# One core, RWKV layer: the mixed streams of k formed and issued ahead of the two low-rank paths

## The chip, the core and the metric

The kernel runs on one core of one Trainium2 chip: TensorE (PE in the rows, its weight loads PEld), VectorE (DVE), ScalarE (ACT), GpSimd (POOL) and a queue that issues the transfers (SP). The metric is the device time of one execution in microseconds, as the median of several; three runs of the kernel before gave 2172.70, 2178.46 and 2179.18 us.

## The reference, cut to what matters

Four post-norm layers work on 256 context tokens and 256 latent tokens of 1024 features: retention, mLSTM, RWKV-7, retention. The change lies at the start of the RWKV layer. There each token stream `u` is mixed with a shifted copy of itself, six times with six weights, and projected:

```
xx = shifted - u
xr, xw, xk, xv, xa, xg = (u + xx * mix[j] for j in range(6))
r, k, v, g = einsum('nbtd,nde->nbte', stack([xr, xk, xv, xg]), w_rkvg)
kk = heads(k * k_k);  kk = kk / max(sqrt(sum(kk * kk)), 1e-12)
wlog = -softplus(-(w0[d] + tanh(xw @ w1[d]) @ w2[d])) - 0.5     # d: two directions
a    = sigmoid(a0[d] + (xa @ a1[d]) @ a2[d])
```

The context is shifted along its sequence, the latents on a grid of rows of 64. The "two low-rank paths" are `tanh(xw @ w1)` and `xa @ a1`, both directions together 128 columns wide each. They are needed only later, when the recurrence over chunks of 64 tokens is prepared; k and its normalised form are needed there too.

## The kernel before

Features lie on partitions (8 tiles of 128), the 512 tokens along the free dimension: 0 to 255 the context, 256 to 511 the latents. `Norm.finish` (lines 103 to 119) of the layer in front writes the RWKV layer's input `h`, first for the context, then for the latents, tile by tile on DVE (lines 108, 110), POOL (108) and ACT (116). `rk_project` (line 1031) then does this:

- `shifted` (1040) forms `xx` for one stream: subtractions on DVE (1037), edges on ACT (1038).
- `mixed` (1068) gives one tile of one mixed stream in float32, on DVE (line 1070), into a slot `rxm`. There are three such slots, and `colb` and `lnpart` of the norm take theirs from the same three.
- `lora` (1084) sends 8 such tiles of a stream through TensorE in plain float32 (line 1087) for each of the two paths, and ACT takes the sums to `tw` and `ta` (1088). Plain float32 matmuls leave two records each in the trace.
- `mix_split` (1073) forms the k stream's tiles and splits each into two exact parts: the high one on ACT (line 288), the low one on DVE (line 289). The tiles are named `szr`, `xk` and `zh` after the slots they take (2, 3 and 3 pairs).
- `first_proj` (268) multiplies them with the first two units of k's weights, three matmuls for each pair (lines 256 to 258): four tiles of output, of the context's 256 tokens first, then of the latents', 96 matmuls for each half.
- The other four tiles of k (numbers 4 to 7) follow over all 512 tokens, 24 matmuls each (`proj`, "pp" in the rows). For each four tiles: copy out (1113), store to memory (1114), times `k_k` into a slot `kkt` (1115; four slots), square (1118), sums over a head (1120), root and reciprocal (1122 to 1124), spread back (1128), multiply (1130), store (1131). A slot `kkt` is free again once its store has landed.

The sums of both paths, `lps`, take two banks of PSUM of a tag "ps" that has two, and keep them until ACT has read them. `rk_rest` (1134) follows with r's mixed stream (line 1144, then 288 and 289) and its projection, and `rk_core` with the recurrence: `prep` (1268; its POOL lines are 1315, 1320 and 1322), `solve` (1363; POOL and DVE in step, lines 1380 and 1381, eight times), `whole`, `step`.

No order is written out by hand here: the framework's scheduler lays the calls of each engine out by a simulation of its own, in the order of the program where nothing else decides. Each engine then works its list off strictly in that order.

Of the kernel before, what the change touches and what calls it, by code (L numbers as in the profile page):

```python
# [16 lines left out]
T = 512  # L17
# [31 lines left out]
class Norm:  # L49
    """The layer's norm of one stream over its features, taken up tile by tile. The sums are of the differences to the  # L50
    mean of the first 128 features, which is within a few standard deviations of the mean."""
# [17 lines left out]
    def add(self, c):  # L69
# [10 lines left out]
        # four partial sums, each on 32 partitions  # L80
# [22 lines left out]
    def finish(self):  # L103
# [16 lines left out]
        # the last layer adds to the latents alone  # L120
# [3 lines left out]
    def late(self):  # L124
        """What the next layer adds to."""
        nc = self.net.nc
        for k in range(KT):
            x = self.x[k]
            nc.gpsimd.tensor_tensor(out=x, in0=x, in1=self.rs, op=OP.mult)
            nc.gpsimd.tensor_scalar(out=x, in0=x, scalar1=self.cs[:, 2, k:k + 1], scalar2=self.cs[:, 3, k:k + 1], op0=OP.mult, op1=OP.add)  # L130


class Net:
# [41 lines left out]
    def filler(self, n=0):  # L175
        """The next piece of what the layer can do at any time."""
        if self.fill and FILL[n]:
            self.ada(*self.fill.pop(0))
# [6 lines left out]
    def open_pw(self, name, bufs=(3, 4, 4), side="right"):  # L185
        """Weights: raw and in their exact parts, on the other side of SBUF."""
# [8 lines left out]
    def open_slots(self, es, name, groups, side="left"):  # L195
        """Slots by what they are for: the tiles of a group take theirs in turn."""
# [3 lines left out]
    def t(self, name, dt=F32, n=512):  # L200
        """A slot of at most 512 columns."""
# [4 lines left out]
    def q(self, name, n=HALF):  # L206
        """A small slot of at most 256 columns."""
# [13 lines left out]
    def pt(self, tag, n=512):  # L221
        """A bank of PSUM."""
# [4 lines left out]
    # ---------------------------------------------------------------- weights  # L227
    def raw(self, src, n):
        """A piece of a weight as [128, 1024 / n, n]."""
# [14 lines left out]
    def unit(self, w, n0, n=256, lo=0, hi=None):  # L244
        """Columns n0.. of w in their exact parts, a pair of [128, n] for each 128 rows."""
# [14 lines left out]
    def proj(self, w, c, lo, hi):  # L260
        """Feature-major product of 128 columns with the tokens lo..hi."""
# [6 lines left out]
    def first_proj(self, jobs, by_k=False, po=4):  # L268
        """proj for a layer's first jobs (w, c, lo): the context's tokens ahead of the latents', or the input's features in turn."""
# [16 lines left out]
    def halves(self, src, h, l, eng=None):  # L286
        """src into its exact parts."""
# [4 lines left out]
    # ---------------------------------------------------------------- adaLN  # L292
    def ada(self, i, pieces, nb=4, slots=None):
        """128 * nb columns of the modulation at a time; slots: a tile of weights, its columns, one of PSUM, one for the transpose."""
# [31 lines left out]
    def make_h(self, i, k, st, src, s, b):  # L326
        """h = src * s + b, the input of layer i, in its exact parts (whole for the RWKV layer)."""
# [34 lines left out]
    # ---------------------------------------------------------------- layer end  # L362
    def add_out(self, i, c, st, ps):
        """x += gate * y for 128 features of one stream."""
# [4 lines left out]
    def out_rows(self, i, w, r0, z, lo0, streams, units=None):  # L369
        """x += gate * (z @ w[r0:r0+512]); z in 4 pairs of tiles of 128 features, from token lo0."""  # L370
# [31 lines left out]
    def log_sigmoid_(self, x, tl):  # L402
        """-(max(-x, 0) + log1p(exp(-|x|))), the logarithm by its atanh series."""
# [22 lines left out]
    def columns(self, ps, parts):  # L426
        """Sums over the partitions of tiles; parts: the columns of 128 of ps that a tile of 128 queries adds to."""
# [3 lines left out]
    def rows(self, col, n, tag="ps"):  # L431
        """Columns of 128 back to n values along the free dimension, the same in every partition."""
# [7 lines left out]
    def rsqrt_rows(self, squares, n, scale, eps, tag="ps"):  # L440
        """(scale * sums over the partitions + eps) ** -0.5 for n columns."""
# [9 lines left out]
    # ---------------------------------------------------------------- retention  # L451
# [37 lines left out]
    def ret_masks(self, h, w384, lg, lgx):  # L489
        """exp(distance * log gamma) summed over the directions, by (query - key): within a stream, latents to context."""  # L490
# [42 lines left out]
    def ret_v(self, h, v, u, w_in):  # L533
        """Half of the values, tokens on partitions."""
# [11 lines left out]
    def ret_values(self, h, qk, v, w_in, w_out, streams, rope, w384, lg, lgx):  # L546
# [4 lines left out]
        # scores of a tile of keys, [keys, queries]  # L551
# [37 lines left out]
        # gates  # L589
# [12 lines left out]
    # ---------------------------------------------------------------- mLSTM  # L602
    def mlstm(self, i, j):
        nc, a = self.nc, self.a
        w_in, w_out = a["ml_w_in"][j], a["ml_w_out"][j]
        with ExitStack() as es:
# [3 lines left out]
            # what goes on into the next layer  # L610
# [12 lines left out]
            def gate_weights(g):  # L623
                """The gates' weights for the convolved and the plain stream, of 4 tiles."""
# [16 lines left out]
            # the convolved stream, that of half the heads by way of memory, and the gates  # L641
# [39 lines left out]
            # the plain stream and the outer gate go by way of memory until their head's turn, as does what the layer adds to  # L681
# [57 lines left out]
    def ml_gates(self, gps, sel, gb, cst):  # L739
        """Rows 32 * direction + head: -G = -max(0, cummax(g)) to memory, g = i - B and exp(-(B + G)) by column."""  # L740
# [42 lines left out]
    def ml_front(self, h, xc, dg, masks):  # L783
        """Both sides of the scores and the decay's part by query."""
        nc, a = self.nc, self.a
        k0 = 4 * h
        # q k' = x (Wq Wk') x'
# [29 lines left out]
        # decay of both directions  # L817
# [10 lines left out]
    def ml_scores(self, h, parts, gcol, ecol):  # L828
        """Decayed scores [keys, queries] of both directions and the inverse denominators."""
# [29 lines left out]
        # denominators  # L859
# [29 lines left out]
    def ml_v(self, h, xmd):  # L889
        """Values without their mean over the head, tokens on partitions."""  # L890
# [67 lines left out]
    def spans(jt, d):  # L958
        """The queries that see key tile jt in direction d."""
# [4 lines left out]
    def rwkv(self, i, j):  # L964
        nc, a = self.nc, self.a
        mm = nc.tensor.matmul
        with ExitStack() as es:
# [26 lines left out]
            # by feature, V by token  # L994
# [3 lines left out]
            # what the steps hold and, above it, what getting their chunks ready takes; the projections' streams lie beside the weights  # L998
# [684 lines left out]
```

## Time and profile before

| | us |
|---|---|
| runs, device time | 2172.70, 2178.46, 2179.18 (median 2178.46) |
| profiled execution, span of its records | 2169.8 |
| PE, DVE, ACT, POOL busy in the span | 1958.8, 1351.0, 942.3, 614.8 |

For the profiled execution the page gives the span alone, not a device time of its own: the median of the runs is 8.7 us above the span (2178.46 - 2169.8). Rows of a stretch ("windows") give the busy time of each engine in it and, behind POOL, the clock that TensorE was granted (1.00 is 2.4 GHz, 0.50 is 1.2 GHz). Rows of groups give busy time and the mean of one instruction in nanoseconds. Rows of the timeline give start, duration, engine, line and what is written from what; in square brackets how long the engine stood idle before it, and what ended that. Matmul records overlap their successor, so the pace of a row of matmuls is read from start to start.

### The profile page before, as it was taken

Reading aid. Unit: us, or ns where it says so; the run is one execution under the profiler, and the core shown is the slowest. Engines: PE = TensorE matmul, PEld = TensorE weight load, DVE = VectorE, ACT = ScalarE, POOL = GpSimd, SP = SyncE. Lnnn points to the kernel's source line nnn. Section 1 sums busy time; section 2 is a strip of 40 time slices with the busy share of each in tenths; the row PEclk is TensorE's granted clock in tenths of the full one; section 3 lists DMA queues with packets and bytes.
Section 4 is the critical chain, followed back from the end, with each engine's and each line's share of the span. In section 5 each row is a group of like instructions: output and inputs, shape, how many; then the busy total and the mean of one; then the engine's idle time right before and its main releaser. Section 6 shows DMA issues by size and latency. Waiting matters only on the chain.

```text
span 2169.8 us, 35237 instructions
## 1 busy us (share of the span) xinstructions
PE 1958.8 (90%) x13594; PEld 1666.2 (77%) x13594; DVE 1351.0 (62%) x2472; ACT 942.3 (43%) x1853; POOL 614.8 (28%) x940
## 2 busy tenths in 40 slices
PE   6999999998999899987999987778878988999996
PEld 5788888877778777775758976677877776999995
DVE  4463535358536477676857467878877665665554
ACT  3342414134435454333435555555756342444433
POOL 1000000007100334324303266655656332311001
PEclk9999999999999999998899998889889999999998
DMA  9333333333545553441235411111222740233331
GB/s 299 118 98 120 114 112 123 92 107 109 193 155 159 169 175 127 136 155 52 76 132 164 148 57 52 40 28 44 63 60 82 236 148 15 78 113 121 117 98 48
DMA packets 241527, 245.94 MB, mean 113 GB/s; under 512 B 30992, under 2 KB 200080, under 8 KB 241360
## 3 DMA queue, kind: packets, MB, share of 16 engines
q1 hardware_dynamic: 241360, 243.70, 35.6%
q8 instruction: 107, 1.75, 0.3%
q14 instruction: 60, 0.49, 0.1%
HBM read 216.26 MB, written 27.39 MB: 112 GB/s over the span
## 4 chain that ended last, share of the span: by engine, by line
PE 65%; DVE 18%; ACT 5%; DMA 4%; issue 4%; POOL 3%; SPq 0%; DVEq 0%; ACTq 0%; POOLq 0%
PE pp L256 15%; PE pp L257 15%; PE pp L258 15%; DVE LS L1381 2%; DVE sol L1380 2%; PE po L257 2%; PE ps L83 2%; PE po L256 2%; PE po L258 2%; DMA raw<-ada_w 1%; ACT bdB L1200 1%; PE ps L308 1%; DVE wl L240 1%; ACT AD L1200 1%; PE g L1330 1%
## 5 line engine op out<-in xcount | busy, mean ns | idle before, releaser
L240 DVE TENSOR_TENSOR wl<-wraw,wh 128x1024 fp32r<-128x1024 f32 x216 | 270.8, 1255 | 202.9 <-ACT wh L238 195.1
L238 ACT ACTIVATE wh<-wraw 128x1024 fp32r<-128x1024 f32 x216 | 228.6, 1059 | 265.8 <-PE pp L257 111.7
L256 PE MATMUL pp<-hA,wh 128*128 128x512 f32 (+1 forms) x704 | 255.4, 365 | 6.6 <-DVE rp L527 3.0
L257 PE MATMUL pp<-hB,wh 128*128 128x512 f32 (+1 forms) x704 | 254.8, 363 | 0.0
L258 PE MATMUL pp<-hA,wl 128*128 128x512 f32 (+1 forms) x704 | 254.6, 363 | 0.1
L256 PE MATMUL pp<-zh,wh 128*128 128x512 f32 (+1 forms) x620 | 216.0, 351 | 10.6 <-ACT zh L288 6.0
L258 PE MATMUL pp<-zh,wl 128*128 128x512 f32 (+1 forms) x620 | 210.8, 340 | 0.0
L257 PE MATMUL pp<-zl,wh 128*128 128x256 f32 (+1 forms) x512 | 169.2, 330 | 3.1 <-DVE zl L289 3.1
L367 DVE SCALAR_TENSOR_TENSOR x<-pp,mod,x 128x256 f32<-128x256 f32 x192 | 87.3, 480 | 132.8 <-PE pp L258 132.4
L256 PEld LDWEIGHTS pp<-hA,wh 128*128 128x128 f32 x704 | 132.5, 189 | 31.5 <-PE pp L258 3.6
L258 PEld LDWEIGHTS pp<-hA,wl 128*128 128x128 f32 x704 | 133.1, 189 | 23.9 <-issue 1.6
L257 PEld LDWEIGHTS pp<-hB,wh 128*128 128x128 f32 x704 | 133.1, 189 | 22.4 <-issue 1.7
L256 PEld LDWEIGHTS pp<-zh,wh 128*128 128x128 f32 x620 | 117.9, 191 | 40.2 <-issue 10.2
L256 PE MATMUL pp<-wh,hA 128*128 128x256 f32 x512 | 145.7, 286 | 2.0 <-ACT wh L238 1.9
L257 PE MATMUL pp<-wl,hA 128*128 128x256 f32 x512 | 144.9, 284 | 0.8 <-DVE wl L240 0.8
L258 PE MATMUL pp<-wh,hB 128*128 128x256 f32 x512 | 144.5, 283 | 0.0
L258 PEld LDWEIGHTS pp<-zh,wl 128*128 128x128 f32 x620 | 118.3, 191 | 20.2 <-issue 7.6
L1380 POOL TENSOR_TENSOR sol<-AD 128x84 f32<-128x84 f32 (+13 forms) x240 | 97.0, 404 | 117.9 <-ACT AD L1200 100.6
L257 PEld LDWEIGHTS pp<-zl,wh 128*128 128x128 f32 x512 | 98.2, 192 | 16.7 <-issue 5.4
L1381 POOL TENSOR_TENSOR AD<-AD,sol 128x84 f32<-128x84 f32 (+13 forms) x240 | 98.0, 408 | 18.2
L256 PEld LDWEIGHTS pp<-wh,hA 128*128 128x128 f32 x512 | 96.9, 190 | 5.9 <-issue 2.7
L257 PEld LDWEIGHTS pp<-wl,hA 128*128 128x128 f32 x512 | 97.3, 190 | 1.7 <-DVE wl L240 1.0
(519 smaller groups left out, 4911.4 us busy)
## 6 DMA issues: line engine op xcount, KB each, us to landing
wraw<-ret_w_in SPq DMA_DIRECT2D x96, 512.0 KB, 3.7
wraw<-ada_w SPq DMA_DIRECT2D x56, 512.0 KB, 4.0
wraw<-ret_w_out SPq DMA_DIRECT2D x32, 512.0 KB, 3.4
wraw<-ml_w_in SPq DMA_DIRECT2D x32, 512.0 KB, 3.8
wraw<-rk_w_rkvg SPq DMA_DIRECT2D x32, 512.0 KB, 3.6
adaw<-ada_w SPq DMA_DIRECT2D x48, 256.0 KB, 4.5
raw<-ada_w SPq DMA_DIRECT2D x16, 512.0 KB, 7.6
wraw<-ml_w_out SPq DMA_DIRECT2D x16, 512.0 KB, 4.7
```

Of the source, the lines that this page charges most:

```text
L83: nc.tensor.matmul(self.sums[32 * j:32 * j + 32, n * HALF:n * HALF + HALF], net.ones[:, 0:32], src, start=c < 4 and n == 0, stop=c >= 4 an ...
L238: nc.scalar.activation(h, t, ACT.Copy)
L240: (nc.gpsimd if self.nsplit % 4 in self.psplit else nc.vector).tensor_tensor(out=l, in0=t, in1=f(h), op=OP.subtract)
L256: mm(ps, lhs[0], rhs[0], start=start, stop=False)
L257: mm(ps, lhs[0], rhs[1], start=False, stop=False)
L258: mm(ps, lhs[1], rhs[0], start=False, stop=stop)
L308: nc.tensor.matmul(ps[32 * j:32 * j + 32, 0:m].rearrange("p (b q) -> p b q", b=nb), self.csil[:, k, :], raws[k // n][:, k % n, j], start=k ...
L367: self.nc.vector.scalar_tensor_tensor(out=x, in0=ps, scalar=self.gate(i, c, st), in1=x, op0=OP.mult, op1=OP.add)
L1200: copy = lambda o, x: nc.scalar.activation(o, x, ACT.Copy)
L1330: mm(g[:, p, 0:192], cat(u["bb"][:, p]), W[:, p], start=True, stop=True)
L1380: eng.tensor_tensor(out=t, in0=A[:, s + 1:, s:s + 1].broadcast_to([128, m, n]), in1=A[:, s:s + 1, lo:hi].broadcast_to([128, m, n]), op=OP. ...
L1381: eng.tensor_tensor(out=A[:, s + 1:, lo:hi], in0=A[:, s + 1:, lo:hi], in1=t, op=OP.add)
```

## The change

The context's and the latents' k streams are formed first, one after the other, and all of `first_proj` is called behind them. The banks for the low-rank sums are taken only then, and `lora` is called once over all 512 tokens instead of once for each stream, which makes 16 tiles of 512 columns and 16 matmuls out of 32 of 256. Apart from this the diff only takes out comments and docstrings.

```diff
         for t, nm in zip(lw, ("rk_w1", "rk_a1")):
             nc.sync.dma_start(t, a[nm])
-        lps = [self.pt("ps") for _ in loras]
         wu = [self.unit(w[1], u * 256) for u in range(2)]
         load_rest()
-        shifted(CTX)
-        lora(slice(0, HALF))
-        mix_split(2, slice(0, HALF))
-        shifted(LAT)
-        lora(slice(HALF, T))
-        mix_split(2, slice(HALF, T))
-        # k and its normalised form
+        for st in (CTX, LAT):
+            shifted(st)
+            mix_split(2, slice(st * HALF, st * HALF + HALF))
+
         first = self.first_proj([(x, cc, 0) for x in wu for cc in range(2)])
+        lps = [self.pt("ps") for _ in loras]
+        lora(slice(0, T))
         for u in range(0, 4, 2):
```

Line numbers of the kernel after are 2 lower from there on (1118 for 1120, 1126 for 1128, 1285 for 1287, 1313 to 1320 for 1315 to 1322).

DVE, from the copy `colb` that ends the statistics of the latents' norm. Before, the mixed tiles (`rxm`) between the norm's own lines 108 and 110 are those of the low-rank paths:

```order
L434 COPY colb<-lncol 128x512
L1070 SCALAR_TENSOR_TENSOR rxm<-xx,cmix,h_8717 128x256 x3
L108 TENSOR_TENSOR x_6104<-x_6104,lndm 128x256
L108 TENSOR_TENSOR x_6105<-x_6105,lndm 128x256
L108 TENSOR_TENSOR x_6108<-x_6108,lndm 128x256
L1070 SCALAR_TENSOR_TENSOR rxm<-xx,cmix,h_8717 128x256
L110 SCALAR_TENSOR_TENSOR lnt<-x_6104,lncs,lnrs 128x256
L110 SCALAR_TENSOR_TENSOR lnt<-x_6105,lncs,lnrs 128x256
L1070 SCALAR_TENSOR_TENSOR rxm<-xx,cmix,h_8717 128x256 x2
```

After, at the same place, they are those of k, and low parts (line 289) stand between them:

```order
L434 COPY colb<-lncol 128x512
L1070 SCALAR_TENSOR_TENSOR rxm<-xx,cmix,h_8717 128x256 x2
L289 TENSOR_TENSOR szr<-rxm,szr 128x256 x2
L1070 SCALAR_TENSOR_TENSOR rxm<-xx,cmix,h_8717 128x256 x3
L108 TENSOR_TENSOR x_6104<-x_6104,lndm 128x256
L108 TENSOR_TENSOR x_6105<-x_6105,lndm 128x256
L108 TENSOR_TENSOR x_6108<-x_6108,lndm 128x256
L289 TENSOR_TENSOR xk<-rxm,xk 128x256
L110 SCALAR_TENSOR_TENSOR lnt<-x_6104,lncs,lnrs 128x256
L289 TENSOR_TENSOR xk<-rxm,xk 128x256 x2
L110 SCALAR_TENSOR_TENSOR lnt<-x_6105,lncs,lnrs 128x256
L1070 SCALAR_TENSOR_TENSOR rxm<-xx,cmix,h_8717 128x256 x2
```

So the exact parts of the context's k stream stand where the low-rank tiles stood, and those move behind the latents' k stream.

PE, in the projection of k's tiles 4 and 5, where the squares of tiles 0 to 3 are summed (`ps<-sq`). Before, no low-rank matmul (line 1087) is left; line 1287 already uses `tw` and `ta`:

```order
L257 MATMUL pp<-zh,wh 128x512
L1120 MATMUL ps<-sq,hs_9177 32x512
L258 MATMUL pp<-zh,wl 128x512
L256 MATMUL pp<-zh,wh 128x512
L257 MATMUL pp<-zh,wh 128x512
L258 MATMUL pp<-zh,wl 128x512
L1287 MATMUL g_10594<-tw,cw_9161 128x128
L1287 MATMUL g_10594<-ta,ca_9162 128x128
L1120 MATMUL ps<-sq,hs_9177 32x512
```

After, the low-rank matmuls stand between those of k, and the four sums come behind ten of them:

```order
L1087 MATMUL ps<-rxm,lw 128x512
L258 MATMUL pp<-zh,wl 128x512
L1087 MATMUL ps<-rxm,lw 128x512
L1118 MATMUL ps<-sq,hs_9177 32x512 x4
L1285 MATMUL g_10544<-tw,cw_9161 128x128
L1285 MATMUL g_10877<-tw,cw_9161 128x128
L1087 MATMUL ps<-rxm,lw 128x512 x3
L256 MATMUL pp<-szr,wh 128x512
```

The other six come later: three ahead of tile 6 and three behind it, among the matmuls that spread the reciprocals back (line 1126).

POOL, at the end of the fourth `solve` of the recurrence. Before, the work of two `prep` calls (lines 1315, 1320, 1322) lies between the solve's steps (1380, 1381), and the next solve follows its end (1383) at once:

```order
L1315 TENSOR_TENSOR th<-th,k 128x512
L1380 TENSOR_TENSOR sol<-AD_11523 128x12
L1320 TENSOR_TENSOR bdA<-th,em 64x4x2x64 x2
L1381 TENSOR_TENSOR AD_11523<-AD_11523,sol 128x2x6
L1322 TENSOR_TENSOR th<-th,r 128x512
L1380 TENSOR_TENSOR sol<-AD_11523 128x6
L1381 TENSOR_TENSOR AD_11523<-AD_11523,sol 128x6
L1383 COPY LS<-AD_11523 128x32x6
L1380 TENSOR_TENSOR sol<-AD_10573 128x30
```

After, that work stands between the two solves:

```order
L1378 TENSOR_TENSOR sol<-AD_11473 128x6
L1379 TENSOR_TENSOR AD_11473<-AD_11473,sol 128x6
L1381 COPY LS<-AD_11473 128x32x6
L1313 TENSOR_TENSOR th<-th,k 128x512
L1300 COPY Dc<-eL_10520 64x8 x2
L1318 TENSOR_TENSOR bdA<-th,em 64x4x2x64 x2
L1320 TENSOR_TENSOR th<-th,r 128x512
L1313 TENSOR_TENSOR th<-th,k 128x512
L1318 TENSOR_TENSOR bdA<-th,em 64x4x2x64 x2
L1320 TENSOR_TENSOR th<-th,r 128x512
L1378 TENSOR_TENSOR sol<-AD_10523 128x30
```

In the sixth and in the seventh solve one `prep` more moves out of the steps in the same way; in the fifth one moves in.

## Rows read from the trace of the kernel before

**Rows 1.** The page's head.
```profile
span 2169.8 us, 35237 instructions
```

**Rows 2.** Stretches: length, busy PE, PEld, DVE, ACT, POOL, granted clock, DMA, GB/s.
```profile
1025.00:1048.00 23.00, 16.91 (x42) 11.10 (x43) 21.30 (x35) 6.47 (x18) 22.17 (x29) 0.57 0.18 69
1048.00:1079.00 31.00, 30.77 (x225) 28.63 (x225) 25.11 (x57) 12.58 (x26) 0.57 (x3) 0.98 0.08 29
...
1100.00:1112.00 12.00, 7.80 (x24) 3.39 (x23) 3.91 (x8) 2.23 (x4) 0.00 (x0) 0.79 0.33 124
...
1120.00:1270.00 150.00, 147.74 (x845) 126.30 (x844) 98.35 (x140) 73.05 (x153) 48.39 (x83) 1.00 0.44 138
1270.00:1720.00 450.00, 358.91 (x3029) 322.70 (x3031) 344.14 (x694) 260.93 (x622) 271.20 (x528) 0.90 0.25 72
```

**Rows 3.** The same view in stretches of 2 us, around the start of k.
```profile
1028.00:1030.00 2.00, 1.19 (x4) 0.65 (x3) 2.00 (x4) 0.00 (x0) 2.00 (x4) 0.86 0.02 4
...
1032.00:1034.00 2.00, 1.27 (x3) 0.90 (x4) 2.00 (x3) 0.60 (x3) 2.00 (x3) 0.50 0.00 0
...
1050.00:1052.00 2.00, 2.00 (x19) 2.00 (x18) 2.00 (x6) 1.04 (x4) 0.00 (x0) 1.00 0.00 0
```

**Rows 4.** Timeline of PE and DVE, 1026 to 1112 us.
```profile
1026.93 2.26 PE L1087 MATMUL ps<-rxm,lw 128*128 128x256 f32 x6
...
1045.46 0.55 DVE L1037 TENSOR_TENSOR xx<-h 128x384 f32<-128x384 f32 x1
...
1062.50 4.48 PE L1087 MATMUL ps<-rxm,lw 128*128 128x256 f32 x20
...
1067.14 0.74 PE L256 MATMUL po<-szr,wh 128*128 128x256 f32 x4 [0.16 <-ACT szr L288]
...
1078.90 0.40 PE L256 MATMUL pp<-szr,wh 128*128 128x512 f32 x1
1079.13 0.40 PE L257 MATMUL pp<-szr,wh 128*128 128x512 f32 x1
...
1084.33 1.05 PE L1120 MATMUL ps<-sq,hs 128*32 128x512 f32 x2
...
1093.63 0.37 PE L1287 MATMUL g<-tw,cw 64*128 64x128 f32 x1
...
1096.59 0.27 PE L1287 MATMUL g<-tw,cw 64*128 64x128 f32 x1
...
1102.81 1.13 PE L1128 MATMUL ps<-rn,chb 32*128 32x512 f32 x4
...
1109.86 1.92 PE L1120 MATMUL ps<-sq,hs 128*32 128x512 f32 x2 [3.42 <-ACT sq L1118]
1111.70 0.80 PE L256 MATMUL pp<-szr,wh 128*128 128x512 f32 x1
```

**Rows 5.** The chain of waits, the store of the first normalised tile.
```profile
1104.69 3.84 DMA mkk<-kkt
```

**Rows 6.** Groups on DVE by shape, 1024 to 1152 us: busy, mean ns, idle before.
```profile
L1070 DVE SCALAR_TENSOR_TENSOR rxm<-xx,cmix,h 128x256 f32<-128x256 f32 x48 | 24.8, 546 | 7.6 <-PE ps L1087 6.2 <-PE ps L437 1.2
L240 DVE TENSOR_TENSOR wl<-wraw,wh 128x1024 fp32r<-128x1024 f32 x12 | 15.0, 1248 | 14.0 <-ACT wh L238 14.0
L1144 DVE SCALAR_TENSOR_TENSOR rxm<-xx,cmix,h 128x512 f32<-128x512 f32 x17 | 12.5, 746 | 0.0
...
L289 DVE TENSOR_TENSOR zh<-rxm,zh 128x256 fp32r<-128x256 f32 x6 | 2.3, 418 | 0.0
```

**Rows 7.** Groups on POOL by shape, 1230 to 1720 us.
```profile
L1320 POOL TENSOR_TENSOR bdA<-th,em 64x512 f32<-64x512 f32 x28 | 39.7, 1418 | 1.4
L1315 POOL TENSOR_TENSOR th<-th,k 128x512 f32<-128x512 f32 x14 | 19.6, 1401 | 15.7 <-ACT th L1313 14.0 <-DVE sol L1380 1.6
L1322 POOL TENSOR_TENSOR th<-th,r 128x512 f32<-128x512 f32 x14 | 17.8, 1270 | 0.5
```

**Rows 8.** Timeline of POOL, start of the fifth solve.
```profile
1487.37 0.25 POOL L1380 TENSOR_TENSOR sol<-AD 128x30 f32<-128x30 f32 x1 [15.87 <-ACT AD L1200]
```

## Prediction, made before the kernel after was run

> **What bounds the kernel now.** I read the span first [rows 1], then the busy times by stretch [rows 2], because a share of the whole span says nothing of a change that touches some 90 us of it. Three things are to be seen there. From 1025 to 1048 us DVE works 21.3 of 23 us and PE only 16.9, at a mean granted clock of 0.57: the latents' norm is being finished on DVE, the low-rank tiles stand between, and PE waits for each. From 1048 to 1079 PE is full (30.8 of 31) at 0.98. From 1100 to 1112 PE falls to 7.8 of 12 at 0.79. From 1120 to 1270, r's and the values' projections, it is full again, 147.7 of 150 at full clock. So whatever brings PE earlier to that stretch is carried through it; whatever is lost on PE while it waits for DVE, or runs at 1.2 GHz, is what the change can win back. Then I read the clock in steps of 2 us [rows 3] and the timeline around k [rows 4].
>
> **The change, part by part.** All durations come from the profiled execution, whose span of 2169.8 us lies 8.7 under the median of the runs; the sum is a difference, taken off the span and the median alike.
>
> *End of first_proj.* Before, its last matmul ends where the next tile starts, at 1078.90 [rows 4]. Its latents' half, 96 matmuls, ran from 1067.14 to 1078.90: 11.8 us, 0.12 each. After, DVE goes through the same norm and the same `xx`, but up to the last `xx` it forms 11 mixed tiles and 11 low parts in place of 15 mixed tiles. That is 11 x 0.546 + 11 x 0.418 = 10.6 us for 15 x 0.546 = 8.2 [rows 6], 2.4 more, of which the 1.7 us that DVE stood idle in 1025 to 1048 [rows 2] can take a part. The last `xx` ended at 1045.46 + 0.55 = 1046.0 [rows 4], so now at 1046.7 to 1048.4. Behind it come 5 mixed tiles, 5 low parts and 3 wide low-rank tiles of 0.746: 2.7 + 2.1 + 2.2 = 7.0. The last low part is ready at 1053.7 to 1055.4, and 12 matmuls follow it (1.5): DVE alone allows an end at 1055 to 1057.
>
> PE: the context's half starts at about 1027, where the low-rank path started [rows 4]. It needs 11.8 us at full clock, twice that, 23.5, at 0.50. Fed tile by tile, it is done by 1046 in the one case and by 1050.5 in the other. The latents' half then ends 11.8 later, at 1057.8 or 1062.3. I take 1059.
>
> For the clock the row of 1032 to 1034 shows 0.50 while PE's records cover 1.27 of 2 us, and 1050 to 1052 shows 1.00 with PE full [rows 3]. The Trainium skill, TensorE: Matmul & The Clock Gate, section What's actually happening, says that the throttled state is the default and that activity releases it. By that rule the steadily fed context half gets the full clock, and the end is 1057.8; by the row of a PE two thirds busy it stays at half, and the end is 1062.3. Both lie in the range below.
>
> The 0.418 of a low part was taken with POOL nearly idle (0.57 of 31 us), and 11 of them now fall where POOL is busy 22.2 of 23 [rows 2]. Unmeasured there; I bound it by no change below and by twice the time above, 4.6 us on DVE, which would put the end at 1061.5 at most, and I keep the lower value. The Trainium skill, GPSIMD Engine Reference, section 1. Specifications, states that GpSimd shares its SBUF interfaces with VectorE and contends with its instructions that have two SBUF inputs, which a low part has. By that the upper value is the nearer one and the gain 2 to 3 us smaller.
>
> *The low-rank matmuls.* They go from 32 of 256 columns to 16 of 512. Ten narrow ones took 4.48 us [rows 4], 0.448 each; twice that is 0.90. A 512-column float32 matmul, line 1120, took 1.05. So 14.3 to 16.8 us, I take 15: the columns stay the same, nothing is saved on PE. DVE forms 16 tiles of 0.746 for 32 of 0.546 [rows 6], 11.9 for 17.5. Not on the path after 1059, so I count it at nothing; it is cover for the low parts of the weights (1.25 each), which now fall in between.
>
> *From there to the start of k's tile 7.* PE has: low-rank 15; tiles 4 to 6, 72 matmuls of 0.23 (1079.13 - 1078.90), 16.6; four sums of squares at 1.05, 4.2; three spreads at 1.13 / 2, 1.7; the 32 small ones of line 1287, which from 1093.63 to 1096.86 with one sum among them took 3.2 - 1.05 = 2.2 [rows 4]. Together 39.7, so tile 7 starts at 1098.7. Before, it started at 1111.70 with one sum and one spread more already done (1.6): 1110.1 like for like. Gain 11.4. Two things make it up: 1078.9 - (1059 + 15) = 4.9 from the front, and 6.5 from the gap at 1104 to 1110. In that gap all four spreads stand together, the first normalised tile must be stored (3.84 [rows 5]) before DVE gets a free `kkt`, DVE, ACT and PE wait in turn, 3.42 us on PE alone, and the sum behind it runs at 1.92 instead of 1.05 [rows 4]. After, three low-rank matmuls, the small ones and two spreads, about 2.7 + 2.2 + 1.1 = 6.0 us, stand in that wait.
>
> *What is late next.* Two more squares wait for the stores of the second and third normalised tile, 0 to 3.84 us on PE; I take 2 off. The wait is in DVE's queue: behind it stand r's mixed tiles and low parts, which r's projection needs only behind tile 7. The banks of the low-rank sums now delay the sums of squares until ACT has read `tw`; ten low-rank matmuls stand ahead of them anyway, so nothing is added. SP's list keeps its transfers, in a slightly other order; no cost. `tw` and `ta` come some 25 us later, and are used by line 1287 alone, placed behind them.
>
> 11.4 - 2 = 9.4 us. From 1120 on PE is full, so it arrives at the recurrence (1270 to 1720, PE 359 of 450), where engines wait for each other in a chain that shifts as a whole; its order changes in places. 2178.46 - 9.4 = 2169.1, as a span 2160.4.
>
> **Rivals.**
> 1. *The gap of tile 7 stays* (the store still ends a wait that nothing covers): 4.9 - 0 to 2 is left, 2174 to 2176. For it: the same store and the same four slots. Against: 6 us of other matmuls now stand behind the first spread.
> 2. *The recurrence gives it back*, because a chain off PE sets its start: 2178, no change. For it: PE is only 80% busy there. Against: PE full for 150 us ahead of it.
> 3. *Slower, by POOL's order in the recurrence.* The `prep` work of four calls moves out of the solves to behind them and one moves in, net three; each is 1.40 + 2 x 1.42 + 1.27 = 5.5 us [rows 7]. If the next solve waits for it, that is 16.5, less 9.4: 7 slower, 2185.6. It decides where POOL is the last to be ready. Against: before the fifth solve POOL stood idle for 15.87 us, waiting for ACT [rows 8], room for two calls (11.0); and the solve that they leave gets shorter.
> 4. *More than forecast*: end of first_proj at 1055, no new wait: 11.4 + 3.8 = 15.2, 2163.
>
> **How the numbers follow.** A measurement of this kernel tells 0.3%, 6.5 us, from no change; so faster means under 2171.9. The forecast (6 to 13 us of gain) gets 0.45; rival 4 gets 0.11; rival 1 0.17; rival 2 0.14; rival 3 0.13, with other mishaps of the new order in the recurrence. Faster: 0.42 + 0.11 + 0.05 (rival 2 where the order helps) = 0.58. Slower: 0.12. Same: 0.30. Range: 2159 (rival 4 and 4 us that the recurrence may win) to 2182 (rival 2 and part of rival 3), leaving a tenth on either side. The forecast's own range is 2165 to 2173.
>
> **What would show it.** First_proj's last matmul at 1055 to 1062 by the timeline; mixed tiles of 512 columns behind it at 0.75 us; low-rank matmuls at 0.9 to 1.05 us between those of k; PE idle under 3 us between 1060 and 1120; tile 7 starting at 1096 to 1103, and r's projection and the first solve some 9 us earlier than before. It is wrong if the context's half ends behind 1051, if low parts under POOL take 0.8 us, if PE waits over 4 us at tile 7 or for r's parts, or if the first solve is early and the last is not.

## Result and the profile after

The kernel after ran in 2152.76 us, before in 2178.36 on the same chip: 25.6 us between the medians. The ratio is 0.9889 (95% interval 0.9875 to 0.9903), by which 24.2 us of 2178.36 are gained where 9.4 were forecast. A second time, on another chip, the ratio was 0.9913 (0.99 to 0.9926), 18.9 us. Every ratio here is against the kernel before on the same chip, and gains are taken from the ratio. The time lies below the predicted range.

First the stretches that the prediction read [rows 2] and the clock behind the norm [rows 3], in the same columns, kernel after:

```profile
1025.00:1048.00 23.00, 16.97 (x108) 15.88 (x108) 21.45 (x37) 10.17 (x27) 22.13 (x29) 0.83 0.15 58
1060.00:1120.00 60.00, 59.91 (x237) 36.30 (x236) 41.51 (x55) 23.20 (x36) 1.22 (x2) 1.00 0.36 119
1100.00:1112.00 12.00, 12.00 (x41) 6.25 (x41) 7.38 (x10) 7.09 (x11) 1.22 (x2) 1.00 0.33 114
1120.00:1270.00 150.00, 147.34 (x890) 128.07 (x889) 89.03 (x127) 73.80 (x155) 52.19 (x91) 0.99 0.42 132
1270.00:1720.00 450.00, 358.60 (x3090) 321.30 (x3089) 346.42 (x706) 260.29 (x622) 264.14 (x520) 0.90 0.26 76
...
1028.00:1034.00 6.00, 6.00 (x34) 6.00 (x33) 6.00 (x11) 2.30 (x7) 6.00 (x10) 0.58 0.01 3
1034.00:1040.00 6.00, 5.04 (x38) 4.42 (x37) 6.00 (x10) 3.30 (x10) 5.13 (x8) 1.00 0.00 1
...
1050.00:1052.00 2.00, 2.00 (x13) 2.00 (x11) 2.00 (x5) 1.24 (x3) 2.00 (x4) 0.52 0.63 231
```

From 1025 to 1048 PE is busy as long as before (16.97 for 16.91 us), but at a mean clock of 0.83 instead of 0.57 and with the matmuls of k. The gap from 1100 to 1112 is gone: PE works 59.91 of 60 us from 1060 to 1120, at full clock. In the recurrence nothing shows in the sums: 358.60 us of PE for 358.91, the same clock.

Then the timeline of PE [rows 4] and the groups on VectorE [rows 6], kernel after:

```profile
1028.75 1.20 PE L256 MATMUL po<-szr,wh 128*128 128x256 f32 x4
...
1044.90 0.74 PE L256 MATMUL po<-szr,wh 128*128 128x256 f32 x4 [0.17 <-ACT szr L288]
1048.66 0.39 PE L257 MATMUL po<-szr,wh 128*128 128x256 f32 x1 [3.02 <-DVE szr L289]
...
1061.22 2.73 PE L1087 MATMUL ps<-rxm,lw 128*128 128x512 f32 x6
...
1081.00 1.06 PE L1118 MATMUL ps<-sq,hs 128*32 128x512 f32 x8
...
1091.78 2.84 PE L1087 MATMUL ps<-rxm,lw 128*128 128x512 f32 x6
1094.55 2.33 PE L1126 MATMUL ps<-rn,chb 32*128 32x512 f32 x4
...
1098.56 0.50 PE L256 MATMUL pp<-szr,wh 128*128 128x512 f32 x1
```

```profile
L1070 DVE SCALAR_TENSOR_TENSOR rxm<-xx,cmix,h 128x512 f32<-128x512 f32 x16 | 11.6, 740 | 5.8 <-PE ps L1087 5.8
...
L289 DVE TENSOR_TENSOR xk<-rxm,xk 128x256 fp32r<-128x256 f32 x6 | 4.1, 717 | 0.0
...
L289 DVE TENSOR_TENSOR zh<-rxm,zh 128x256 fp32r<-128x256 f32 x6 | 2.3, 411 | 0.0
```

First_proj ends where the low-rank matmuls start, at 1061.22, the four sums stand at 1081.0, and tile 7 starts at 1098.56. VectorE's wide tiles waited 5.8 us for PE, not the other way round.

The profiled executions differ already ahead of the change: the copy `colb` that ends the norm's statistics starts at 1024.51 in before and at 1026.47 in after. So I count from it. Three rows with four times cut the rest: that copy, the first and the last solve's end (a memset on VectorE, eight times), and the last update of a state (56 times). In each fence the rows of one kernel; "first and last start" stand behind the durations.

Before:
```profile
1024.51 0.44 DVE L434 COPY colb<-lncol 128x512 f32<-128x512 f32 x1 [2.51 <-POOL lncol L170]
...
L1384 DVE MEMSET LS<- x8: 85/85/85, 1266.0 to 1704.7; 128x32 f32 x8
...
L1441 DVE TENSOR_TENSOR S<-pp,Dc x56: 425/427/428, 1298.9 to 1737.0; 64x256 f32<-64x256 f32 x56
```
After:
```profile
1026.47 0.44 DVE L434 COPY colb<-lncol 128x512 f32<-128x512 f32 x1 [2.50 <-POOL lncol L170]
...
L1382 DVE MEMSET LS<- x8: 85/85/85, 1256.4 to 1695.7; 128x32 f32 x8
...
L1439 DVE TENSOR_TENSOR S<-pp,Dc x56: 425/427/429, 1291.0 to 1722.2; 64x256 f32<-64x256 f32 x56
```

From the copy to the first solve's end 241.5 us became 229.9 (11.6 gained), between the two solves 438.7 became 439.3, from there to the last update 32.3 became 26.5 (5.8), and from there to the end of the span (2169.8 and 2149.6) 432.8 became 427.4 (5.4). So the front, the part that the change rewrites, gave 11.6 in this execution. Of the other 10.6, all that shows in these stretches shows behind the last solve (11.2, less 0.6 ahead of it), where the change touches no code.

What differs there? VectorE and ScalarE, before, from the last transpose of the solve to the copy of Q, with which `whole` begins (L1200 and L1201 are its copies on either engine; in brackets the wait and what ended it):

```profile
1706.03 1.91 DVE L1387 STREAM_TRANSPOSE O<-LS 128x1024 f32<-128x1024 f32 x1
1707.86 0.65 DVE L1480 TENSOR_REDUCE rs<-ysq 128x8 f32<-128x512 f32 x1
1708.57 0.68 DVE L1451 TENSOR_TENSOR Y<-pp,Y 64x512 f32<-64x512 f32 x1
1714.08 0.20 DVE L1482 RECIPROCAL rs<-rs 128x8 f32<-128x8 f32 x1 [4.82 <-ACT rs L1481]
...
1716.50 0.69 DVE L1201 COPY Q<-ps 32x512 f32<-32x512 f32 x1
...
1707.98 4.45 ACT L1200 ACTIVATE bdB<-O 32x512 f32<-32x512 f32 x4 [1.89 <-DVE O L1387]
1712.45 1.28 ACT L1481 ACT_TABLE_LOAD   x1
1713.75 0.30 ACT L1481 ACTIVATE rs<-rs,gneps 128x8 f32<-128x8 f32 x1
1714.07 0.59 ACT L1200 ACTIVATE Q<-ps 32x512 f32<-32x512 f32 x1
```

After, the same place (line numbers 2 lower):

```profile
1697.02 1.92 DVE L1385 STREAM_TRANSPOSE O<-LS 128x1024 f32<-128x1024 f32 x1
1698.86 0.65 DVE L1476 TENSOR_TENSOR Y<-Y,mu 128x512 f32<-128x512 f32 x1
1704.00 0.69 DVE L1199 COPY Q<-ps 32x512 f32<-32x512 f32 x1 [4.49 <-ACT Q L1198]
...
1698.97 4.38 ACT L1198 ACTIVATE bdB<-O 32x512 f32<-32x512 f32 x4 [2.43 <-DVE O L1385]
1703.38 0.59 ACT L1198 ACTIVATE Q<-ps 32x512 f32<-32x512 f32 x1
```

Before, part of a `finish` (line 1471) stands between the solve and its `whole`: VectorE waits for a root on ScalarE that stands behind four copies and loads its table first, and Q starts 8.6 us behind the end of the transposes. After, that finish was done within the solve, and it is 5.1. The wait itself is about as long in both, 4.82 and 4.49 us, because ScalarE's four copies of O stand ahead in both. The 3.5 us lie elsewhere: ScalarE reaches its own copy of Q 4.4 us behind the transposes instead of 6.1, without the table and the root ahead of it, and VectorE's copy starts 0.6 us behind that one instead of 2.4, without the pieces of the finish between. A solve leaves gaps on these engines; which work falls into them is the scheduler's choice. The calls of the recurrence are the same and are traced in the same order; on VectorE 349 of the 1352 instructions traced behind `rk_project` stand four places or more elsewhere among themselves than before, on TensorE 1122 of 5107.

### The profile page after: what moved, and what is told of

Same layout as the page of the kernel before. It is cut to its first block, busy times and chain, and to the rows that moved or that the text cites. A ratio compares the mean times of both kernels' runs of the same rounds, so it can differ in the third digit from the quotient of the medians.

```text
span 2149.6 us, 35145 instructions
## 1 busy us (share of the span) xinstructions
PE 1947.1 (91%) x13562; PEld 1654.9 (77%) x13562; DVE 1344.2 (63%) x2456; ACT 941.9 (44%) x1851; POOL 612.7 (29%) x940
## 5 line engine op out<-in xcount | busy, mean ns | idle before, releaser
L238 ACT ACTIVATE wh<-wraw 128x1024 fp32r<-128x1024 f32 x216 | 228.5, 1059 | 263.5 <-PE pp L257 119.3
L1379 POOL TENSOR_TENSOR AD<-AD,sol 128x84 f32<-128x84 f32 (+13 forms) x240 | 101.8, 424 | 18.1
```

The source lines that it names most:

```text
L238: nc.scalar.activation(h, t, ACT.Copy)
L1379: eng.tensor_tensor(out=A[:, s + 1:, lo:hi], in0=A[:, s + 1:, lo:hi], in1=t, op=OP.add)
```

## Experiments

**Order and front apart.** The front is what the change rewrites in `rk_project`; the order is how each engine's instructions behind it are laid out. Theory O: the front gives what the first solve shows, the rest comes from the order. To hold an order, each engine's instructions that are traced behind `rk_project` were chained in the order of a list taken from the other kernel (`k` and `last` are neighbours in it; the dependence carries no semaphore):

```diff
             h, xx = self.rk_project(K, B, p1, p0, load_rest)
+            self.mark = len(nc.cur_bb.bb.instructions)
...
+        pin(tc, nc.cur_bb.bb.instructions[net.mark:])
...
+            if j:
+                tc.add_manual_dep(ins[k], ins[last].name, info, reason="order")
```

front_old_order: the new front with the old list.

> The changed front, but from rk_rest on each engine's instructions stand among themselves in the order of the kernel before. Theory O (the front gives 9.5 to 11.5 us, as the first solve of the traces shows, and the rest of the gain comes from another order in the recurrence and at its end): 2166 to 2170 us, ratio 0.994 to 0.996, and the lag behind the kernel before stays at 8 to 12 us from 1120 us to the end. Rival H (a head start that the recurrence turns into more by itself, whatever its order): 2151 to 2156, ratio 0.988 to 0.990. Rival M (the front only pays together with the order that was made for it): over 2172.

old_front_new_order: the old front with the new list.

> The front of the kernel before, but from rk_rest on each engine's instructions stand among themselves in the order of the changed kernel. Theory O: the 20.2 us between the two profiled spans less 9.5 to 11.5 of the front leave 9 to 11, so 2164 to 2170 us, ratio 0.994 to 0.997, gained between 1430 and 1760 us. Rival H: 2176 to 2180, no change. Rival M: slower than before or the same, since that order was laid out for instructions that come 10 us earlier.

Measured: 2160.93 and 2159.35 us where before is 2174.49, ratios 0.994 (0.9925 to 0.9954) and 0.9931 (0.9917 to 0.9945). That is 13.1 us for the front alone and 15.0 for the order alone, each at the upper edge of what theory O gave or a little above. Rivals H and M fall. The two do not add up: 28.1 us apart, 24.2 and 18.9 together, so on top of the new front the order brought about 11 and 6 us. The rows as above, front_old_order:

```profile
1026.39 0.44 DVE L434 COPY colb<-lncol 128x512 f32<-128x512 f32 x1 [2.50 <-POOL lncol L170]
...
L1382 DVE MEMSET LS<- x8: 85/85/85, 1253.0 to 1692.6; 128x32 f32 x8
...
L1439 DVE TENSOR_TENSOR S<-pp,Dc x56: 425/427/428, 1287.7 to 1724.7; 64x256 f32<-64x256 f32 x56
```

old_front_new_order:

```profile
1029.19 0.44 DVE L434 COPY colb<-lncol 128x512 f32<-128x512 f32 x1 [2.50 <-POOL lncol L170]
...
L1384 DVE MEMSET LS<- x8: 85/85/85, 1268.9 to 1704.3; 128x32 f32 x8
...
L1441 DVE TENSOR_TENSOR S<-pp,Dc x56: 425/427/428, 1301.8 to 1731.1; 64x256 f32<-64x256 f32 x56
```

With its order held, the recurrence takes a head start over unchanged: 439.5 us between the solves, 32.1 to the last update, 432.6 to the end, as before within 0.8 (only one execution of each kernel is profiled; A in the table below differs by 2.1 between two of the changed kernel). With the new order alone the front is 1.8 us shorter, the solves 3.2, the two pieces behind them 5.5 and 4.2.

All kernels in this measure (us, from the same rows and the span of each; A from the copy to the first solve's end, B to the last solve's end, C to the last update, D to the end):

| | A | B | C | D | ratio (95%) |
|---|---|---|---|---|---|
| before | 241.5 | 438.7 | 32.3 | 432.8 | 1 |
| after | 229.9 | 439.3 | 26.5 | 427.4 | 0.9889 (0.9875 to 0.9903) |
| after_again | 227.8 | 438.4 | 26.4 | 428.7 | 0.9913 (0.99 to 0.9926) |
| front_old_order | 226.6 | 439.5 | 32.1 | 432.6 | 0.994 (0.9925 to 0.9954) |
| old_front_new_order | 239.7 | 435.5 | 26.8 | 428.6 | 0.9931 (0.9917 to 0.9945) |
| narrow_behind_old_order | 235.3 | 439.4 | 31.1 | 432.1 | 0.9973 (0.9963 to 0.9983) |
| wide_ahead_old_order | 234.8 | 442.7 | 31.2 | 432.1 | 0.9968 (0.9957 to 0.9979) |
| narrow_by_path_old_order | 230.7 | 439.5 | 32.6 | 432.9 | 0.994 (0.9918 to 0.9961) |
| narrow_by_path_free | 232.6 | 435.4 | 30.5 | 432.6 | 0.9941 (0.9926 to 0.9955) |
| wide_ahead_free | 235.2 | 438.7 | 30.8 | 431.5 | 0.9959 (0.9946 to 0.9972) |
| old_front_new_order_early | 239.5 | 444.8 | 31.1 | 434.7 | 1.0016 (1.0004 to 1.0028) |
| old_front_new_order_late | 242.0 | 445.1 | 26.5 | 428.3 | 0.9971 (0.9957 to 0.9984) |
| old_front_new_order_1541 | 241.9 | 446.3 | 26.6 | 429.2 | 1.0011 (1 to 1.0022) |
| old_finish_behind_q | 240.6 | 439.0 | 28.9 | 433.8 | 0.9991 (0.9981 to 1.0001) |
| new_front_mixed_order | 228.1 | 436.7 | 26.8 | 429.8 | 0.988 (0.986 to 0.99) |
| mixed_order_q_first | 226.7 | 439.8 | 26.0 | 427.5 | 0.9892 (0.9878 to 0.9905) |

**The front in parts**, all with the old order held. narrow_behind_old_order:

```diff
-        lora(slice(0, T))
+        lora(slice(0, HALF)); lora(slice(HALF, T))
```

> As front_old_order, but the low-rank paths behind first_proj are called for 256 tokens twice, with 32 mixed tiles and 32 matmuls of 256 columns. Theory O with the working of the prediction (the width saves nothing on TensorE, the place does it; VectorE has 5.6 us more in a stretch that it does not bound): within 2 us of front_old_order, tile 7 of k at 1096 to 1104. Rival W (the width gives part of it, since VectorE bounds 1060 to 1100 once the low-rank tiles stand there together): 3 to 6 us slower than front_old_order, with TensorE waiting for mixed tiles.

wide_ahead_old_order:

```diff
-        for st in (CTX, LAT):
-            shifted(st)
-            mix_split(2, slice(st * HALF, st * HALF + HALF))
-
-        first = self.first_proj([(x, cc, 0) for x in wu for cc in range(2)])
+        shifted(CTX)
+        mix_split(2, slice(0, HALF))
+        shifted(LAT)
         lps = [self.pt("ps") for _ in loras]
         lora(slice(0, T))
+        mix_split(2, slice(HALF, T))
+        first = self.first_proj([(x, cc, 0) for x in wu for cc in range(2)])
```

> As front_old_order, but the low-rank paths over all 512 tokens stand ahead of the latents' k stream, so that they cannot fill the gap ahead of tile 7. Theory O with the working of the prediction (4.9 us from a TensorE that is fed earlier, 6.5 from the gap): the gap of 3 to 6 us ahead of tile 7 is there again and 3 to 5 us are gained, 2173 to 2176 us. Rival G (the gap is worth nothing by itself, because the time comes from elsewhere): as front_old_order within 2 us. Rival P (the place ahead of the latents' stream leaves TensorE waiting for the mixed tiles, and its clock down): 2178 or more.

Both lost about half of the gain: at 0.9973 and 0.9968, 5.9 and 7.0 us are left of it. The first speaks for rival W by its time, but its trace for something else. Its PE from 1088 on:

```profile
1088.59 2.42 PE L1087 MATMUL ps<-rxm,lw 128*128 128x256 f32 x10
1090.94 1.07 PE L1118 MATMUL ps<-sq,hs 128*32 128x512 f32 x8
...
1101.18 1.13 PE L1126 MATMUL ps<-rn,chb 32*128 32x512 f32 x4
1104.23 2.57 PE L1126 MATMUL ps<-rn,chb 32*128 32x512 f32 x4 [1.92 <-DVE kkt L1128]
1110.12 1.91 PE L1118 MATMUL ps<-sq,hs 128*32 128x512 f32 x2 [3.33 <-ACT sq L1116]
```

The four sums wait until 1090.94, 60.5 us behind the copy where front_old_order has 52.2. My reading: both banks of "ps" hold low-rank sums until nearly all 32 matmuls are done; the four spreads then stand together again, and the gap of 3.33 us ahead of the next sum is the old one [rows 4]. With the same 256 columns, path by path, the first bank comes free after half of them:

```diff
-                for k in range(KT):
-                    mm(ps[:, sl], w[:, k], mixed(m, k, sl), start=k == 0, stop=k == KT - 1)
+                for sk in range(2 * KT):
+                    k, s2 = sk % KT, slice(sk // KT * HALF, sk // KT * HALF + HALF)
+                    mm(ps[:, s2], w[:, k], mixed(m, k, s2), start=k == 0, stop=k == KT - 1)
```

> As narrow_behind_old_order (256 columns, behind first_proj), but path by path: both halves of the first path, then both of the second, so that the first bank is read and free after half of the matmuls. Theory B (there it was not the width: both banks of the sums stayed taken until nearly all 32 matmuls were done, the sums of squares came at 1091 instead of 1079 and the gap ahead of tile 7 was back): within 3 us of front_old_order, which stood at 2160.9 us, ratio 0.994 to 0.9955. Rival W (width: 32 mixed tiles of 0.55 us for 16 of 0.75, 5.6 us more on VectorE, on the path): 5 us or more behind front_old_order, ratio 0.996 to 0.9975.

0.994 (0.9918 to 0.9961), the ratio of front_old_order. Theory B holds: the sums are back at 53.4 us behind the copy, and tile 7 starts at 70.6 (front_old_order 71.8, narrow_behind 81.6), though with up to 3.7 us more of matmuls left behind it. So what narrow_behind lost is put down to when the banks come free and what stands in tile 7's wait. A smaller price of the width is not excluded: up to the first solve this kernel gained 10.8 us, front_old_order 14.9, and the ratio's interval is wide. In wide_ahead the gap shrank to 1.60 us and 6.7 us were gained up to the first solve, more than the 3 to 5 forecast; rivals G and P fall.

**The order in parts**, old front: the new list up to, or from, a place where both lists have done the same instructions on every engine, at about 1637 us. In short (the lists themselves are stored in the kernels):

```diff
-list = {e: old[e] for e in engines}
+list = {e: new[e][:cut[e]] + old[e][cut[e]:] for e in engines}   (early)
+list = {e: old[e][:cut[e]] + new[e][cut[e]:] for e in engines}   (late, 1541)
```

> The kernel before, its front too; only from rk_rest to about 1637 us (between the sixth and the seventh solve) each engine's instructions stand in the changed kernel's order, behind that in the old one. old_front_new_order had won 3.2 us by 1640 and 15 by 1780. Theory T (the order at the last two solves and behind them makes most of it): 2 to 5 us gained, ratio 0.9977 to 0.999. Rival E (the early part makes it, by bringing the last solve nearer): 10 to 15 us, ratio 0.993 to 0.995.

> The kernel before, its front too; only behind about 1637 us each engine's instructions stand in the changed kernel's order. Theory T: the steps of the seventh group, the sums of one finish and the copies of whole run within the last solve instead of behind it, so 10 to 12 us are gained, ratio 0.9945 to 0.9955; the last solve itself ends no earlier, and the gain appears between 1700 and 1770 us. Rival E: 0 to 4 us, since without the head start of the early part the moved work has to wait.

1.0016 and 0.9971: neither as expected. B is 6 us longer in both, C and D are as in the new order where the late part is new (26.5 and 428.3) and nearly the old ones where it is old. The tail came as theory T said; what lies ahead lost. Another place to cut:

> As old_front_new_order_late, with the change from the old to the new order at about 1541 us instead of 1637. Both halves cut at 1637 lost 5 to 7 us right behind the cut. Theory S (that loss belongs to the seam, where work that one order had put ahead is put behind by the other; the gain belongs to the last two solves and what follows): 10 to 14 us, ratio 0.9935 to 0.9955. Rival E (the order ahead of 1541 us is needed for it): 3 to 8 us, ratio 0.9965 to 0.9985.

1.0011 (1 to 1.0022), theory S falls by its number: B is 7.6 us longer, C and D again gain 9.3. So what is gained behind the last solve belongs to the late part, in all seven executions (of six kernels) that have it. It is not won for nothing. B hides how the two orders spread the solves; the times between their ends (us, from the eight memsets) show it:

| | 1 to 2 | 2 to 3 | 3 to 4 | 4 to 5 | 5 to 6 | 6 to 7 | 7 to 8 |
|---|---|---|---|---|---|---|---|
| before | 89.3 | 60.1 | 61.8 | 44.0 | 76.4 | 59.4 | 47.6 |
| after | 92.2 | 54.7 | 42.7 | 72.1 | 58.4 | 58.5 | 60.7 |
| old_front_new_order_early | 90.6 | 55.0 | 42.7 | 72.1 | 57.9 | 76.8 | 49.8 |
| old_front_new_order_late | 89.7 | 60.5 | 62.0 | 44.8 | 76.4 | 50.8 | 60.9 |
| old_front_new_order_1541 | 89.8 | 60.6 | 59.0 | 44.1 | 74.0 | 58.7 | 60.1 |

In the new order the last interval is 13.1 us longer, since work that stood behind the last solve (the finish above) now stands ahead of it, and the six intervals ahead are 12.4 shorter in sum. A list cut in two has one without the other: late and 1541 have the long last interval without all of the short ones (late has 8 us back in the sixth), and early pays 76.8 us in the sixth. So each part needs the other. Which instructions cost this no run shows.

old_finish_behind_q moves seven instructions in the old list, on VectorE (DVE) and ScalarE (ACT):

```diff
-DVE: L1480 L1451 L1482 L1476 L1483 L1477 L1478 L311 L1201(Q) L314 L314 L1201(bdB) L1201(bdB)
+DVE: L1451 L311 L1201(Q) L314 L314 L1201(bdB) L1201(bdB) L1480 L1482 L1476 L1483 L1477 L1478
-ACT: L1481 L1200(Q) L1200 L1200 L1200 L1200
+ACT: L1200(Q) L1200 L1200 L1200 L1200 L1481
```

> The kernel before with its own order, but for seven instructions: on VectorE the six of the finish that stand between the end of the last solve and the copy of Q (the sum of squares, the reciprocal, the mean, two differences and a product) go behind the three copies of whole, and on ScalarE the root that loads its table goes behind the copies too. In before the copy of Q started 8.6 us after the solve's last transpose, 5 of them in the wait for the root; in old_front_new_order 5.1. Theory T (what stands between the last solve and its whole sets the end): Q 3 to 5 us earlier, and 3 to 5 us gained at the end, ratio 0.9975 to 0.9985. Rival F (the finish itself becomes the late one, since its transposes on TensorE and its product are needed for the output's second half): Q earlier, the end the same or up to 3 us later.

Q started 5.1 us behind the transposes instead of 8.6, C fell by 3.4 us, D rose by 1.0. The ratio, 0.9991 (0.9981 to 1.0001), is 2.0 us, at the edge of what these runs tell and under the 3 to 5 us of theory T; the 1.0 us in D is of the kind that rival F named. So these seven instructions are 3.4 of the 5.8 us that C gained in after. That the rest of C, and D, come from the seventh group's steps, which now fall into the last solve, is argued and was not isolated.

**Does the order follow from an early front?** Two of the fronts again, nothing held:

```diff
-        pin(tc, nc.cur_bb.bb.instructions[net.mark:])
```

> As narrow_by_path_old_order, but nothing is pinned: the scheduler lays out the recurrence itself. On GpSimd it leaves the prep work at the end of the solves as before the change does, and 33 of 732 instructions stand four places or more from the old order, 94 from the changed kernel's. Theory C (the good order belongs to one layout, not to an early front): ratio 0.993 to 0.9955, as pinned (0.994). Rival E (an early front brings the gain with it): 0.988 to 0.991, as the changed kernel.

> As wide_ahead_old_order, but nothing is pinned; here too the scheduler's order of the recurrence stays close to the old one. Theory C: ratio 0.995 to 0.998, as pinned (0.9968). Rival E: with 7 us of the front there, a part of the order's gain too, 0.991 to 0.994.

0.9941 (0.9926 to 0.9955) and 0.9959 (0.9946 to 0.9972): theory C. Two fronts that start k as early, one of them as good as the changed one, bring no such order; C is 30.5 and 30.8, D 432.6 and 431.5, for 32.3 and 432.8 before. The order's gain comes from the one layout that the scheduler found for this text. These two also show that holding an order costs nothing to speak of: 0.9941 free for 0.994 held, 0.9959 for 0.9968.

**Better ones**, from the new front:

```diff
+list = {e: old[e][:cut[e]] + new[e][cut[e]:] for e in engines}   (cut at about 1300 us)
```

> The changed front; the old order up to about 1300 us (the projections of r and of the values and the first grams), the changed kernel's order behind that. With the old order throughout, the new front had won 14.8 us by the first solve, with its own order 11.5. If the two gains add up: 13.1 + 15.0 = 28 us, ratio 0.987, 2146 where before is 2174.5, 2 to 3 us better than the changed kernel (ratio 0.9889). If the order behind 1300 us does not depend on that and the 3 us are lost again by the first solves: as the changed kernel, 0.9885 to 0.989.

mixed_order_q_first, besides, on ScalarE behind the last solve:

```diff
-ACT: L1198(bdB<-O) L1198(bdB<-O) L1198(bdB<-O) L1198(bdB<-O) L1198(Q)
+ACT: L1198(bdB<-O) L1198(bdB<-O) L1198(Q) L1198(bdB<-O) L1198(bdB<-O)
```

> As new_front_mixed_order; besides, ScalarE's copy of Q behind the last solve stands behind two instead of four copies of O. VectorE's copy of Q waited 4.5 us for it there (1707.5 to 1712.0, four copies of 1.1 us). If whole sets the end: 2.2 us earlier, 2144 to 2149 where before is 2174 to 2176, ratio 0.986 to 0.9875. If the copies of O, now later, end the same wait: as new_front_mixed_order, 0.988.

> The changed kernel once more, on the same chip as the two versions made from it: 0.9875 to 0.9903 of before, as the first time. It tells whether new_front_mixed_order (0.988) and mixed_order_q_first are faster than it by more than their intervals.

0.988 (0.986 to 0.99): not told from the changed kernel. With ScalarE's copy of Q ahead of two copies of O, Q comes 2.3 us earlier behind the solve (VectorE waits 2.21 for 4.49), and 2150.43 us were the lowest median on that chip, where the changed kernel had 2155.73; the intervals (0.9878 to 0.9905, 0.99 to 0.9926) overlap. The 28 us that the two gains would add up to were not reached: 0.988 is 26.1.

## Why the prediction was wrong

*The step that failed* is the last of the sum: "it arrives at the recurrence ..., where engines wait for each other in a chain that shifts as a whole; its order changes in places". The first half holds, shown by front_old_order: with the order held, 14.9 us at the first solve are 14.4 at the end. The second half got no term in the sum. I had compared POOL's order alone, priced it as a loss (rival 3) and let the range hold 4 us in its favour. Measured alone, on the old front, the order was worth 15.0 us, as much as the front (13.1; the intervals overlap). Of the 14.7 that its trace shows, 9.7 lie behind the last solve. There the trace of before has a table load, a root and pieces of a finish between a solve and its `whole`, worth 3.4 us of C when moved, and the order of the changed kernel does not; the rest is not isolated. That this change brought such an order is luck as far as the prediction goes: two other early fronts did not.

*End of first_proj*: forecast 1059 in the times of the trace before, 19.9 earlier. It came at 1061.22, 34.8 us behind the copy instead of 54.4: 19.6. The number is right in part by luck. The context's half, at 0.58 at first and at 1.00 from 1034 on, ended 18.1 us behind the copy, ahead of both cases (1046 and 1050.5 are 21.5 and 26.0). Then TensorE waited 3.02 us for the latents' first low part, and its clock fell behind that wait, 0.52 from 1050 to 1052; the sum had the latents' half in 11.8 us without either, and it took 16.3. In front_old_order, the same front, the clock is 1.00 from 1050 to 1052:

```profile
1050.00:1052.00 2.00, 2.00 (x19) 2.00 (x19) 2.00 (x6) 1.24 (x3) 2.00 (x3) 1.00 0.37 139
```

There first_proj ends 32.4 us behind the copy. Over the eight profiled executions with `lora` behind it the end lies between 32.4 and 35.7, the later the more of the latents' 96 matmuls ran at the slow pace, 0.21 us apart instead of 0.12 (1 to 25 of them). Low parts beside POOL cost 0.95 us or 0.41 (below), between the two bounds; 0.95 is past the 0.8 that was given as a sign of being wrong, but did not move the end out of its range.

*Low-rank matmuls*: 15 forecast. In after one stretches the start of its neighbours by 0.86 (1068.19 to 1069.28, less 0.23 for the other matmul), 13.8 for 16.

*Tile 7*: 85.6 us behind the copy like for like (1110.1 - 1024.5), now 72.1 (1098.56 - 1026.47): 13.5 where 11.4 was forecast. *The 2 us for two more waits on stores* did not come: PE is 59.91 of 60 us busy from 1060 to 1120. These two terms are mis-sized, 9.4 for 13.5. Up to the first solve the changed kernel kept 11.6 in one execution and 13.7 in another, and front_old_order 14.9.

*Rival 1* fell, and narrow_behind shows what it would have been. *Rival 2* fell. *Rival 3* named the right place for surprises, but not the right sign. The prep work does stand behind the fourth solve now, and the fifth still waits for ScalarE, 10.08 us for 15.87 [rows 8], as the argument against it said:

```profile
1457.20 1.27 POOL L1313 TENSOR_TENSOR th<-th,k 128x512 f32<-128x512 f32 x1 [5.46 <-ACT th L1311]
1458.55 2.59 POOL L1318 TENSOR_TENSOR bdA<-th,em 64x512 f32<-64x512 f32 x2
1461.22 1.60 POOL L1320 TENSOR_TENSOR th<-th,r 128x512 f32<-128x512 f32 x1
1472.90 0.25 POOL L1378 TENSOR_TENSOR sol<-AD 128x30 f32<-128x30 f32 x1 [10.08 <-ACT AD L1198]
```

*Rival 4* had the size of the front and the cause half right: no new wait; an earlier first_proj came only where the clock stayed up.

## What to carry to other kernels

Where a scheduler lays out the program, a change has two effects: what it does where it stands, and another order everywhere behind. Hold the old order and the first can be measured by itself; only that part may be credited to the change, and the other can be kept or dropped on its own. The two need not add up. A forecast has to look at every engine's order at the ends of serial pieces (here: a solve and its `whole`) and ask what now stands between them.

## Not expected of the hardware

Where two-input operations of VectorE (256 columns) and POOL's operations met, which engine paid depended on POOL's operation. VectorE and POOL of the kernel after, start and duration first:

```profile
1031.81 0.95 DVE L289 TENSOR_TENSOR xk<-rxm,xk 128x256 fp32r<-128x256 f32 x1
...
1040.01 0.75 DVE L289 TENSOR_TENSOR zh<-rxm,zh 128x256 fp32r<-128x256 f32 x2
...
1024.53 0.55 POOL L130 TENSOR_SCALAR x<-x,lncs 128x256 f32<-128x256 f32 x1
...
1030.79 4.32 POOL L108 TENSOR_TENSOR x<-x,lndm 128x256 f32<-128x256 f32 x5
...
1039.81 1.21 POOL L130 TENSOR_SCALAR x<-x,lncs 128x256 f32<-128x256 f32 x1
```

Beside POOL's subtractions of two tiles (line 108, 0.86 each) a low part took 0.95 us, where 0.418 was its time with POOL nearly idle [rows 6]. Beside its one-input line 130 two low parts took 0.75 together, no longer than that, and that line took 1.21 instead of the 0.55 that it took with VectorE idle at 1024.53. The contention that the Trainium skill states (GPSIMD Engine Reference, section 1. Specifications) is in this trace, with 0.95 for 0.418. The forecast had only VectorE pay for it.
